# A two-layer decoder trunk on one core: squares of the last tiles, residual sums, two compression weights and one gate pair are placed differently

## Chip, core and metric

The kernel runs on one core of a Trainium2 chip. The metric is the device time of one execution, in microseconds (us). The core has TensorE (PE) for matrix products, VectorE (DVE), ScalarE (ACT) and GpSimd (POOL) for work on elements, and SyncE (SP), which here only starts DMA transfers. Each engine takes its instructions strictly in the order of its own queue; an instruction that must wait holds up all that stand behind it.

## What is computed

Two layers, each of two blocks with a norm before and after. Cut to what matters here:

```python
def hybrid_layer(x, ...):
    hn = rms_norm(x, norm_g[0])
    (nsa_q, k_c, v_c, ..., sb_q, sb_k, sb_v, merge_g) = split_columns(hn @ w_in)
    kc = compress_blocks(k_c, cmp_pe[0], cmp_w1[0], cmp_w2[0])   # gelu(flat @ w1) @ w2
    vc = compress_blocks(v_c, cmp_pe[1], cmp_w1[1], cmp_w2[1])
    y_nsa = nsa_attention(..., kc, vc, ...) @ w_nsa_o
    y_sb = stick_breaking_attention(...) @ w_sb_o
    gate = jax.nn.sigmoid(merge_g)
    mixed = (gate[..., :D_MODEL] * y_nsa + gate[..., D_MODEL:] * y_sb) @ w_out
    x = x + rms_norm(mixed, norm_g[1])
    hf = rms_norm(x, norm_g[2])
    ff = jnp.square(jax.nn.relu(hf @ w_ff1)) @ w_ff2
    return x + rms_norm(ff, norm_g[3])
```

The sequence has 512 positions, the model 1024 channels (eight tiles of 128), the feed-forward 4096, everything in float32.

## The kernel before

**Layout.** Activations lie with channels on the 128 partitions and the 512 positions along the row. Every large product is made of three: a float32 operand is split into a rounded part and a rest (`hi` and `lo`, in the names `w_hi`/`w_lo` for weights, `ah`/`al` and others for activations), and PE adds hi x hi, hi x lo and lo x hi (`three`, lines 185 to 187; `product`, lines 479 to 483).

**Weights.** `Weight` (line 146) loads 128x1024 values into `w_raw` (two buffers, DMA started by SP), ACT copies them rounded into `w_hi` (line 157), and the rest `w_lo` is made in one of two ways. As a rule POOL subtracts (line 162). With `sub="dma"`, ACT writes the negated rounded copy into `w_lo` (line 159) and a DMA issued from POOL adds the weight from memory onto it (line 160). `w_hi` and `w_lo` have four buffers.

**Compression.** `Compress.steps` (line 371) runs the first compression product in four weight portions for the keys (`ck`) and four for the values (`cv`); the bits of `CKM` and `CVM` in `PLAN` say which portions take the DMA way: 2 is portion 1 of `ck`, 1 is portion 0 of `cv`. `gelu` and `finish` follow; PE's products there are `cmp_t` (line 389) and `cmp_o` (line 409).

**What sets the order.** PE's order is the program's, written by hand: a filler (`Filler`, line 421) hands out a number of projection products between the steps of the attention (`PLAN` holds the numbers). On the other engines and queues a scheduler orders the instructions, under the limits of the buffer pools: a tile can be written when an earlier user of its buffer is done.

**Merge loop** (line 937). For each of the eight tiles m: two groups of products `y`, DVE multiplies each with its sigmoid (line 947), adds, and splits. The gates of tile 7 are projected inside this loop: at m = 1 both projections are added to the filler and all 48 products run.

**Tails** (`tail`, line 242). There are four: attention and feed-forward of each layer. A tail computes the last five of the eight tiles in two halves of 256 positions (`products`, `evacuate`). Each tile's squares are added by DVE into one sum (`sq_add`, line 237), which `rstd_fin` (line 209) sums over the partitions with a product by `ones` on PE (line 212) and turns into 1/rms (`Rpost`, lines 217 to 222). `residual` (line 282) makes for each of the eight tiles `pn` (DVE, line 291), the new `x` (line 292) and its split into `ah` (ACT, line 226) and `al` (DVE, line 227). The first three tails go on into the next block (`nxt` is set): their old `x` comes by DMA into buffers of the tag `sig` (line 277; six buffers, shared with gates and rope tables; the feed-forward tail has `x` in place), and PE starts the next block's first products, `head`, in pieces (`head_step`): k = 0 and 1 of the first half, then `rstd_fin` of the second half's `Rpost`, then the rest. The last tail has no next block and already gives PE one square tile apart (line 214).

Of the kernel before, what the change touches and what calls it, by code (L numbers as in the profile page):

```python
# [12 lines left out]
ALU = mybir.AluOpType  # L13
# [9 lines left out]
}  # L23
GN = 5
# [25 lines left out]
def layer_kernel(ctx, tc, xT, pos, gvec, tri, consts, smalls, w_in, w1, w_o, w_out, ff1, ff2, out):  # L50
# [11 lines left out]
    def big(tag, name, dt=F32):  # L62
        return sp.tile([P, T], dt, tag=tag, bufs=BUFS[tag], name=name)
# [145 lines left out]
    def rstd_fin(R, acc, c, more=None, tag="t"):  # L209
        n = c.stop - c.start  # L210
        ss = psum(tag, "ss")[:, 0:n]
        E.matmul(ss, ones, acc, start=True, stop=more is None)
        if more is not None:
            E.matmul(ss, ones, more, start=False, stop=True)
        v = half("var")
        y = R[:, c]
        S.activation(y, ss, AF.Ln, scale=1.0 / D, bias=eps_c)
        V.tensor_scalar(v, ss, 1.0 / D, EPS, ALU.mult, ALU.add)
        S.activation(y, y, AF.Exp, scale=-0.5)
        V.tensor_tensor(acc, y, y, ALU.mult)  # L220
        V.scalar_tensor_tensor(v, acc, -0.5, v, ALU.mult, ALU.mult)
        V.scalar_tensor_tensor(y, v, 1.5, y, ALU.add, ALU.mult)
# [19 lines left out]
    def tail(l, n, mixed, acc, load, acts, prev, src, nxt, head):  # L242


        group = range(KT - GN, KT)
        last_sq = []
        na = new_acts() if nxt is not None else None
        R = big("R", "Rpost")
        R2 = big("R", "Rpre") if nxt is not None else None
# [7 lines left out]
        def evacuate(hf, i):  # L257
            c = HALVES[hf]
            m, ps = group[i], pst[i][:, c]
            if prev is None:  # L260
                V.tensor_copy(mixed[m][:, c], ps)
            else:
                V.tensor_tensor(mixed[m][:, c], ps, prev[m][:, c], ALU.add)
            if nxt is None and (hf, i) == (1, GN - 1):
                last_sq.append(half("last_sq"))
                S.activation(last_sq[0], mixed[m][:, c], AF.Square)
            else:
                sq_add(acc[:, c], ps if prev is None else mixed[m][:, c], False, c, V)
            if nxt is None and hf == 1:
                S.activation(mixed[m][:, c], mixed[m][:, c], AF.Copy, scale=gcol(l, n, m))  # L270
# [11 lines left out]
        def residual(hf, xo):  # L282
            c = HALVES[hf]
            for k in range(KT):
                t = big("t", "pn")[:, 0:256]
                if nxt is None and hf == 1:
                    e = G if k in ENDP else V
                    e.tensor_tensor(t, mixed[k][:, c], R[:, c], ALU.mult)
                    (G if k == 5 else e).tensor_tensor(x[k][:, c], t, xo[k], ALU.add)
                else:  # L290
                    V.scalar_tensor_tensor(t, mixed[k][:, c], gcol(l, n, k), R[:, c], ALU.mult, ALU.mult)  # L291
                    (V if nxt is None and k in (1, 4, 7) else G).tensor_tensor(x[k][:, c], t, xo[k], ALU.add)
                if nxt is not None:
                    xsplit(na[k], x[k], gcol(nxt[0], nxt[1], k), c)
                else:
                    nc.sync.dma_start(out[:, k, c], x[k][:, c])
# [24 lines left out]
        if nxt is None:  # L321
            for m in range(KT - GN):
                S.activation(mixed[m][:, HALVES[1]], mixed[m][:, HALVES[1]], AF.Copy, scale=gcol(l, n, m))
            rstd_fin(R, acc[:, HALVES[1]], HALVES[1], last_sq[0])
            residual(1, xo)
            return None
        head_step(hd, na, HALVES[0], (0, 1))
        rstd_fin(R, acc[:, HALVES[1]], HALVES[1])
        residual(1, xo)
        a2 = squares(0), squares(1)  # L330
        head_step(hd, na, HALVES[0], range(2, KT))
# [139 lines left out]
    def layer(l, acts, R, heads):  # L471
# [465 lines left out]
        for m in range(KT):  # L937
            sig = sigs.pop(m)
            with tc.issue_after(last_exp.ins):
                for s in sig:  # L940
                    S.activation(s, s, AF.Sigmoid)
            wo, ys = early.pop(m, None) or (Weight(w_o[l, m]), {})
            for j, src in enumerate((o_nsa, o_sb)):
                ps, done = ys.get(j) or (psum("o", "y"), 0)
                for k in range(done, 4):
                    three(ps, wo, 4 * j + k, src[k], k == 0, k == 3)
                V.tensor_tensor(sig[j], ps, sig[j], ALU.mult)
            V.tensor_tensor(sig[0], sig[0], sig[1], ALU.add)
            tg = "Q" if m < 6 else "L"
            mh, ml = big(tg, f"mh{m}", F32R), big(tg, f"ml{m}", F32R)  # L950
            split(mh, ml, sig[0])
            merged.append((mh, ml))
            if m == PLAN["GA"]:
                fill.add(*gate_project(gates.pop(0)))
                fill.run(48)
        exp_table()

        mixed = [big("L", f"mix{m}") for m in range(KT)]
# [149 lines left out]
```

## Time and profile before

| | us |
|---|---|
| median of 3 runs | 1613.12 |
| lowest and highest of them | 1608.31 and 1613.18 |
| the profiled execution, its own time | 1610.72 |
| span of its profile, first to last instruction | 1608.8 |
| PE busy in the span | 1528.3 |
| DVE, ACT, POOL busy | 858.1, 748.9, 763.2 |

The profile gives, for each engine, when an instruction ran, and for a wait which instruction ended it. The granted clock (PEclk) is a share of TensorE's full speed: 1.00 is 2.4 GHz and 0.50 is 1.2 GHz. Times inside the execution count from the span's start. The stages in order, layer 0: projections and compression to about 120 us, attention to 335, merge and output product to 412, attention tail to 455, feed-forward to 785, its tail to 835; layer 1 repeats this.

### The profile page before, as it was taken

To read this page: it belongs to the slowest core of one execution; us is meant where nothing else is said; L and a number is where in the kernel's file an instruction comes from. 1 tells how busy PE (TensorE), PEld (TensorE's weight loads), DVE (VectorE), ACT (ScalarE), POOL (GpSimd) and SP (SyncE) were. 2 spreads that over 40 slices of the span, in tenths; PEclk is the share of its full clock that TensorE was granted. 3 is DMA by queue.
4 is the path that set the end of the run, shared out by engine and by line. 5 is a ranking of instruction groups with operands and counts; after the bars stand their busy time and mean duration, and the time that the engine had idled before them with its cause. 6 is when DMAs were issued, how large, how long until landed. Compare 5 with 4: busy or idle time off the path is not lost.

```text
span 1608.8 us, 20693 instructions
## 1 busy us (share of the span) xinstructions
PE 1528.3 (95%) x7810; PEld 1288.8 (80%) x7810; DVE 858.1 (53%) x1495; ACT 748.9 (47%) x1379; POOL 763.2 (47%) x527
## 2 busy tenths in 40 slices
PE   7789999999989999999988899999998999999996
PEld 5667778887978888888976787788878988888886
DVE  6788854355583232314698887534447713232245
ACT  6567754553352322324446777554444523232342
POOL 4574344535544444446546724444464444444452
PEclk9899999999999999999999999999999999999998
DMA  6443312224313233233334512122342132323321
GB/s 195 121 131 92 64 55 77 66 91 145 105 43 104 93 94 103 92 102 121 117 100 131 136 49 66 53 79 71 113 144 92 47 98 92 105 92 97 100 92 53
DMA packets 49331, 153.74 MB, mean 96 GB/s; under 512 B 5952, under 2 KB 12496, under 8 KB 49232
## 3 DMA queue, kind: packets, MB, share of 16 engines
q1 hardware_dynamic: 45888, 140.84, 27.2%
q0 software_dynamic: 3200, 11.55, 4.1%
q8 instruction: 61, 1.00, 0.3%
q14 instruction: 38, 0.31, 0.1%
q10 hardware_dynamic: 144, 0.03, 0.0%
HBM read 148.15 MB, written 4.26 MB: 95 GB/s over the span
## 4 chain that ended last, share of the span: by engine, by line
PE 78%; DVE 12%; ACT 2%; issue 2%; DMA 1%; POOL 1%; DVEq 0%; ACTq 0%; POOLq 0%
PE ff L186 12%; PE ff L187 12%; PE ff L185 12%; PE proj L479 5%; PE proj L483 5%; PE proj L481 5%; PE tail L187 2%; PE tail L186 2%; PE tail L185 2%; PE y L185 2%; PE p_t L720 2%; DVE P L690 2%; PE y L186 2%; PE y L187 2%; DVE pn L291 2%
## 5 line engine op out<-in xcount | busy, mean ns | idle before, releaser
L162 POOL TENSOR_TENSOR w_lo<-w_raw,w_hi 128x1024 fp32r<-128x1024 f32 x204 | 494.6, 2425 | 506.1 <-ACT w_hi L157 493.6
L157 ACT ACTIVATE w_hi<-w_raw 128x1024 fp32r<-128x1024 f32 x226 | 239.1, 1059 | 521.2 <-PE ff L186 371.7
L483 PE MATMUL proj<-ah,w_lo 128*128 128x512 f32 x496 | 198.7, 401 | 1.7 <-POOL w_lo L162 1.7
L479 PE MATMUL proj<-ah,w_hi 128*128 128x512 f32 x496 | 199.2, 402 | 0.9 <-ACT w_hi L157 0.9
L481 PE MATMUL proj<-al,w_hi 128*128 128x512 f32 x496 | 198.9, 401 | 0.0
L185 PE MATMUL ff<-ah,w_hi 128*128 128x512 f32 x448 | 174.3, 389 | 0.0
L186 PE MATMUL ff<-al,w_hi 128*128 128x512 f32 x448 | 174.3, 389 | 0.0
L187 PE MATMUL ff<-ah,w_lo 128*128 128x512 f32 x448 | 174.3, 389 | 0.0
L186 PE MATMUL ff<-hl,w_hi 128*128 128x512 f32 x432 | 168.2, 389 | 0.7 <-DVE hl L181 0.7
L185 PE MATMUL ff<-hh,w_hi 128*128 128x512 f32 x432 | 168.1, 389 | 0.0
L187 PE MATMUL ff<-hh,w_lo 128*128 128x512 f32 x432 | 168.1, 389 | 0.0
L181 DVE TENSOR_TENSOR hl<-relu,hh 128x512 fp32r<-128x512 f32 x64 | 106.8, 1673 | 83.7 <-ACT hh L180 83.5
L483 PEld LDWEIGHTS proj<-ah,w_lo 128*128 128x128 f32 x496 | 94.8, 191 | 19.0 <-POOL w_lo L162 2.1
L479 PEld LDWEIGHTS proj<-ah,w_hi 128*128 128x128 f32 x496 | 95.0, 192 | 17.4 <-ACT w_hi L157 1.1
L481 PEld LDWEIGHTS proj<-al,w_hi 128*128 128x128 f32 x496 | 95.0, 192 | 16.7
L1003 DVE TENSOR_TENSOR ffa<-ff,ffa 128x512 f32<-128x512 f32 x38 | 26.3, 692 | 151.3 <-PE ff L187 151.3
L185 PEld LDWEIGHTS ff<-ah,w_hi 128*128 128x128 f32 x448 | 84.1, 188 | 17.5
L187 PEld LDWEIGHTS ff<-ah,w_lo 128*128 128x128 f32 x448 | 84.1, 188 | 17.3
L186 PEld LDWEIGHTS ff<-al,w_hi 128*128 128x128 f32 x448 | 84.1, 188 | 17.3
L186 PEld LDWEIGHTS ff<-hl,w_hi 128*128 128x128 f32 x432 | 81.1, 188 | 17.9 <-DVE hl L181 1.1
L185 PEld LDWEIGHTS ff<-hh,w_hi 128*128 128x128 f32 x432 | 81.1, 188 | 17.0
L187 PEld LDWEIGHTS ff<-hh,w_lo 128*128 128x128 f32 x432 | 81.1, 188 | 16.6
(311 smaller groups left out, 3401.3 us busy)
## 6 DMA issues: line engine op xcount, KB each, us to landing
w_raw<-in_ff_dram SPq DMA_DIRECT2D x128, 512.0 KB, 3.5
w_raw<-in_w_in_dram SPq DMA_DIRECT2D x69, 512.0 KB, 3.6
w_lo<-in_w_in_dram POOLq DMA_DIRECT2D x18, 512.0 KB, 7.7
w_raw<-in_w_dram SPq DMA_DIRECT2D x16, 512.0 KB, 3.6
w_raw<-in_w_o_dram SPq DMA_DIRECT2D x16, 512.0 KB, 3.5
w_raw<-in_w_out_dram SPq DMA_DIRECT2D x16, 512.0 KB, 3.7
x<-in_xT_dram SPq DMA_DIRECT2D x8, 256.0 KB, 6.8
w_lo<-in_w_dram POOLq DMA_DIRECT2D x4, 512.0 KB, 7.0
```

The lines of the kernel that those rows point to most:

```text
L157: S.activation(h, raw, AF.Copy)
L162: (sub or G).tensor_tensor(l, raw, h.bitcast(F32), ALU.subtract)
L181: V.tensor_tensor(lo, src, hi.bitcast(F32), ALU.subtract)
L185: E.matmul(ps, w.hi(k), ah, start=first, stop=False)
L186: E.matmul(ps, w.hi(k), al, start=False, stop=False)
L187: return E.matmul(ps, w.lo(k), ah, start=False, stop=last)
L291: V.scalar_tensor_tensor(t, mixed[k][:, c], gcol(l, n, k), R[:, c], ALU.mult, ALU.mult)
L479: E.matmul(ps, w.hi(k), ah, start=(k == 0), stop=False)
L481: E.matmul(ps, w.hi(k), al, start=False, stop=False)
L483: E.matmul(ps, w.lo(k), ah, start=False, stop=(k == KT - 1))
L690: V.tensor_scalar(pr[h], pr[h], sm4[:, h:h + 1], None, ALU.mult)
L720: E.transpose(pt[:, P * h:P * h + P], pend[j][0][h][:, P * kt:P * kt + P], ident)
```

## The change

Four edits:

1. **Squares.** In the three tails with a next block, the squares of the last five tiles in the second half are no longer added by DVE. ACT writes them into buffers of the tag `sig` (two halves of 256 in each, so three buffers) and PE sums all five with a product by `ones` each, behind that of the sum so far.
2. **Residual sums.** The engine expression of the new `x` is turned round. For the last tail it selects the same engines as before; for the three tails with a next block all sixteen sums move from POOL to DVE.
3. **Compression weights.** `CKM` and `CVM` become 0: all eight portions have their `w_lo` from POOL's subtraction.
4. **Gate pair.** The first projection of gate 7 runs at m = 0, the second at m = 1, 24 products each.

```diff
-    ... "CKM": 2, "CVM": 1, ...
+    ... "CKM": 0, "CVM": 0, ...
@@ rstd_fin
         E.matmul(ss, ones, acc, start=True, stop=more is None)
-        if more is not None:
-            E.matmul(ss, ones, more, start=False, stop=True)
+        for i, m in enumerate(more or ()):
+            E.matmul(ss, ones, m, start=False, stop=i == len(more) - 1)
@@ tail
-        last_sq = []
+        last_sq, pairs = [], []
@@ evacuate
             if nxt is None and (hf, i) == (1, GN - 1):
                 last_sq.append(half("last_sq"))
                 S.activation(last_sq[0], mixed[m][:, c], AF.Square)
+            elif nxt is not None and hf == 1:
+                if i % 2 == 0:
+                    pairs.append(big("sig", "sq2"))
+                last_sq.append(pairs[-1][:, 256 * (i % 2) : 256 * (i % 2) + 256])
+                S.activation(last_sq[-1], ps if prev is None else mixed[m][:, c], AF.Square)
             else:
                 sq_add(acc[:, c], ps if prev is None else mixed[m][:, c], False, c, V)
@@ residual
-                    (V if nxt is None and k in (1, 4, 7) else G).tensor_tensor(x[k][:, c], t, xo[k], ALU.add)
+                    (G if nxt is None and k not in (1, 4, 7) else V).tensor_tensor(x[k][:, c], t, xo[k], ALU.add)
@@ end of tail
-            rstd_fin(R, acc[:, HALVES[1]], HALVES[1], last_sq[0])
+            rstd_fin(R, acc[:, HALVES[1]], HALVES[1], last_sq)
...
-        rstd_fin(R, acc[:, HALVES[1]], HALVES[1])
+        rstd_fin(R, acc[:, HALVES[1]], HALVES[1], last_sq)
@@ merge loop
-            if m == PLAN["GA"]:
+            if m == 0:
                 fill.add(*gate_project(gates.pop(0)))
-                fill.run(48)
+            if m < 2:
+                fill.run(24)
```

PE at the end of the attention tail of layer 0, between the second and the third step of `head`, before:

```order
L187 MATMUL head<-ah_3915,w_lo 128x256
L212 MATMUL ss<-macc,ones 128x256
L185 MATMUL head<-ah_3917,w_hi 128x256
L186 MATMUL head<-al_3918,w_hi 128x256
L187 MATMUL head<-ah_3917,w_lo 128x256
```

and the same place after:

```order
L187 MATMUL head<-ah_3913,w_lo 128x256
L212 MATMUL ss<-macc,ones 128x256
L214 MATMUL ss<-sq_4162,ones 128x256 x2
L214 MATMUL ss<-sq_4265,ones 128x256 x2
L214 MATMUL ss<-sq_4318,ones 128x256
L185 MATMUL head<-ah_3915,w_hi 128x256
```

Five products are new there; the numbers are only those of buffers. DVE in the same tail from the first half's `Rpost` on, before (`pn` is a normed tile, `x` the new residual, `mix` a tile copied out of the product's bank, `macc` the sum of squares):

```order
L291 SCALAR_TENSOR_TENSOR pn<-mix_3765,gv,Rpost 128x256
L291 SCALAR_TENSOR_TENSOR pn<-mix_3766,gv,Rpost 128x256
L291 SCALAR_TENSOR_TENSOR pn<-mix_3767,gv,Rpost 128x256
L291 SCALAR_TENSOR_TENSOR pn<-mix_3768,gv,Rpost 128x256
L237 TENSOR_TENSOR macc<-macc,sq 128x256
L291 SCALAR_TENSOR_TENSOR pn<-mix_3769,gv,Rpost 128x256
L227 SCALAR_TENSOR_TENSOR al_3914<-x_4122,gv,ah_3913 128x256
L261 COPY mix_3770<-tail_3971 128x256
L237 TENSOR_TENSOR macc<-macc,sq 128x256
L291 SCALAR_TENSOR_TENSOR pn<-mix_3770,gv,Rpost 128x256
L261 COPY mix_3771<-tail_3972 128x256
L227 SCALAR_TENSOR_TENSOR al_3916<-x_4123,gv,ah_3915 128x256
```

and after, from the third `x` on (four `pn`, a copy and two `x` stand ahead):

```order
L297 TENSOR_TENSOR x_4122<-pn,x_old 128x256
L297 TENSOR_TENSOR x_4123<-pn,x_old 128x256
L296 SCALAR_TENSOR_TENSOR pn<-mix_3767,gv,Rpost 128x256
L261 COPY mix_3768<-tail_3969 128x256
L296 SCALAR_TENSOR_TENSOR pn<-mix_3768,gv,Rpost 128x256
L227 SCALAR_TENSOR_TENSOR al_3912<-x_4120,gv,ah_3911 128x256
L296 SCALAR_TENSOR_TENSOR pn<-mix_3769,gv,Rpost 128x256
L296 SCALAR_TENSOR_TENSOR pn<-mix_3770,gv,Rpost 128x256
L297 TENSOR_TENSOR x_4124<-pn,x_old 128x256
L297 TENSOR_TENSOR x_4125<-pn,x_old 128x256
L227 SCALAR_TENSOR_TENSOR al_3914<-x_4121,gv,ah_3913 128x256
L261 COPY mix_3769<-tail_3970 128x256
```

The sums of squares have left DVE, the sums `x` stand there, and the second `al` stands behind eight `pn`, six `x` and two copies. Behind the last row follow the seventh `x`, an `al`, the eighth `x`, two `al`, a copy and three `al`. POOL in the compression stage of layer 0, before:

```order
L343 TENSOR_TENSOR qr<-q,cosT 128x512
L160 DMA w_lo<-in_w_dram 128x1024
L143 TENSOR_TENSOR qpl<-q,qph 128x512
L162 TENSOR_TENSOR w_lo<-w_raw,w_hi 128x1024 x4
L343 TENSOR_TENSOR qr<-q,cosT 128x512
L160 DMA w_lo<-in_w_dram 128x1024
L143 TENSOR_TENSOR qpl<-q,qph 128x512
L162 TENSOR_TENSOR w_lo<-w_raw,w_hi 128x1024 x2
```

and after:

```order
L348 TENSOR_TENSOR qr<-q,cosT 128x512
L162 TENSOR_TENSOR w_lo<-w_raw,w_hi 128x1024
L143 TENSOR_TENSOR qpl<-q,qph 128x512
L162 TENSOR_TENSOR w_lo<-w_raw,w_hi 128x1024 x4
L348 TENSOR_TENSOR qr<-q,cosT 128x512
L162 TENSOR_TENSOR w_lo<-w_raw,w_hi 128x1024
L143 TENSOR_TENSOR qpl<-q,qph 128x512
L162 TENSOR_TENSOR w_lo<-w_raw,w_hi 128x1024
```

Each DMA issue has become a subtraction in its place. Two further moves follow from the buffers of the tag `sig`: on SP the old `x` of a tail's second half is loaded behind the feed-forward weights instead of among the output weights, and the rope tables of layer 1 are set up at the end of layer 0's feed-forward tail instead of in its attention tail.

## Rows read from the trace of the kernel before

**Rows 1.** Busy time by stage: stage; its us; PE, PEld, DVE, ACT, POOL; PEclk, DMA.

```profile
425.00:460.00 35.00, 28.98 (x223) 28.34 (x222) 29.44 (x47) 14.83 (x33) 19.65 (x18) 0.90 0.20 65
```

**Rows 2.** PE's waits, whole span: waiting <- releaser: us in total, times, longest.

```profile
PE cmp_h L379 <- DMA w_lo<-in_w_dram: 10.4, 3, 8.8
PE ss L212 <- DVE macc L237: 8.2, 2, 4.1
...
PE ss L212 <- DVE facc L237: 5.7, 2, 5.0
```

**Rows 3.** Timeline of PE in the tails: start, us, instruction, [idle before <- releaser].

```profile
444.39 0.39 PE L186 MATMUL head<-al,w_hi 128*128 128x256 f32 x1 [1.90 <-DVE al L227]
444.62 0.28 PE L187 MATMUL head<-ah,w_lo 128*128 128x256 f32 x1
...
445.68 0.28 PE L187 MATMUL head<-ah,w_lo 128*128 128x256 f32 x1
450.08 0.79 PE L212 MATMUL ss<-macc,ones 128*128 128x256 f32 x1 [4.12 <-DVE macc L237]
...
809.66 0.79 PE L212 MATMUL ss<-facc,ones 128*128 128x256 f32 x1 [4.95 <-DVE facc L237]
```

**Rows 4.** Short stretches, columns as in rows 1: read PE busy and PEclk.

```profile
388.90:392.30 3.40, 3.40 (x10) 2.67 (x9) 2.03 (x2) 1.58 (x2) 1.16 (x2) 0.52 0.62 208
...
450.10:453.70 3.60, 3.60 (x15) 3.42 (x16) 2.73 (x8) 2.93 (x8) 0.24 (x1) 0.51 0.59 186
...
808.70:815.50 6.80, 5.84 (x25) 5.66 (x26) 6.26 (x16) 4.51 (x13) 1.05 (x2) 0.50 0.25 80
```

**Rows 5.** Chain of work in the attention tail: start, us, engine, result, line.

```profile
429.00 0.43 PE ss L212 x2
...
440.46 2.40 DVE macc L237
...
444.74 0.40 DVE al L227
...
446.02 0.33 DVE macc L237
...
447.55 2.15 DVE al L227
...
450.08 1.22 PE ss L212 x2
```

**Rows 6.** Timeline of DVE: the ends of the first half's 1/rms.

```profile
431.56 0.43 DVE L222 SCALAR_TENSOR_TENSOR Rpost<-var,Rpost 128x256 f32<-128x256 f32 x1
...
792.45 0.42 DVE L222 SCALAR_TENSOR_TENSOR Rpost<-var,Rpost 128x256 f32<-128x256 f32 x1
```

**Rows 7.** Timeline of POOL in the attention tail: two weight splits.

```profile
440.18 2.40 POOL L162 TENSOR_TENSOR w_lo<-w_raw,w_hi 128x1024 fp32r<-128x1024 f32 x1
...
446.89 2.52 POOL L162 TENSOR_TENSOR w_lo<-w_raw,w_hi 128x1024 fp32r<-128x1024 f32 x1
```

**Rows 8.** Timeline of ACT in the attention tail: the third weight's rounding.

```profile
444.37 1.05 ACT L157 ACTIVATE w_hi<-w_raw 128x1024 fp32r<-128x1024 f32 x1
```

**Rows 9.** Timeline of PE in the compression stages of both layers.

```profile
67.71 0.47 PE L379 MATMUL cmp_h<-w_lo,bhl 128*64 128x256 f32 x1 [8.83 <-DMA w_lo<-in_w_dram]
96.21 0.28 PE L409 MATMUL cmp_o<-cmp_ht,sml 128*64 128x32 f32 x1 [4.82 <-issue]
...
856.04 0.28 PE L378 MATMUL cmp_h<-w_hi,bhl 128*64 128x256 f32 x1
...
890.55 0.32 PE L409 MATMUL cmp_o<-cmp_ht,sml 128*64 128x32 f32 x1 [2.89 <-DVE cmp_ht L400]
```

**Rows 10.** Timeline of PE and ACT in the merge loop of layer 0.

```profile
388.06 0.47 PE L185 MATMUL y<-onh,w_hi 128*128 128x512 f32 x1 [2.40 <-DVE sig L947]
...
383.26 1.06 ACT L157 ACTIVATE w_hi<-w_raw 128x1024 fp32r<-128x1024 f32 x1 [4.84 <-DMA w_raw<-in_w_out_dram]
```

**Rows 11.** DMA issues of the page: transfer, count, KB each, median us to landing.

```profile
x<-in_xT_dram SPq DMA_DIRECT2D x8, 256.0 KB, 6.8
```

2 rows, old and new, of the table PLAN are left out of this document.

## Prediction

> **What bounds the kernel now.** I read the stages first, then PE's waits, then the timelines around them. PE is busy 1528.3 of 1608.8 us, so time is won where PE stands idle or runs at half its clock, and an edit on another engine counts only if PE waits for that engine there. The list of waits [rows 2] names three that the change can touch: the second half's `ss` waiting for DVE's sum of squares in the two attention tails (8.2 us in two waits) and in the feed-forward tail with a next block (4.95 of 5.7 us), and the compression waiting for a weight that comes by a DMA (8.8 us once).
>
> The attention tail of layer 0 is the clearest [rows 1]: of 35 us PE works 29 and DVE 29.4. Its chain [rows 5] runs from the first half's `ss` through DVE to the second half's `ss`. In it two sorts of DVE rows stand beside each other: an `al` takes 0.40 and a `macc` 0.33, but one `macc` takes 2.40 and one `al` 2.15. On POOL a weight split runs from 440.18 for 2.40 and another from 446.89 for 2.52 [rows 7]: the long DVE rows lie on them. I call this a lock: a DVE instruction on two tiles of SBUF that meets a split costs 2.0 to 2.4 us in place of 0.33 to 0.40. PE pays twice [rows 3]: 1.90 us before the second step of `head`, and 4.12 before `ss`. Behind that wait PE runs at 0.51 of its clock until 453.7 [rows 4], the 1.2 GHz level; for 2.4 us after `ss` has ended this costs another 1.2. The feed-forward tail has one wait of 4.95 and the low clock till 815.5.
>
> **Tails: squares and residual sums.** These two edits act on one chain and are costed together. DVE loses five adds of 0.33 behind Rpost and gets sixteen sums of 0.33 from POOL. POOL loses the sums, so its splits now run when their rounded weight is ready, not behind the sums. PE gets five pairs of products by `ones`, 0.43 us each at full clock (`ss` x2 [rows 5]), six with the old one: 2.6 us. At the low clock one pair took 1.22 [rows 5]. ACT writes the squares itself.
>
> Rpost is ready at 432.0 [rows 6]. From there DVE's new order puts eight `pn`, two `al`, two copies and six `x` up to the second `al`: 10 x 0.40 + 8 x 0.33 = 6.7, so 438.7 without locks. PE is ready for that step at 442.5 (444.39 less 1.90). Each split that meets the queue adds about 2.4. Two give 443.5, three 445.9. PE then needs 1.57 for the step (to 445.96, where the wait of 4.12 begins) and 2.6 for the six sums. The last square comes behind the eighth `x`, 1.4 + 0.8 us after the second `al`, and is no later than PE. So `ss` ends at 446.7, 447.7 or 450.05 with no, two or three locks. Before, it ended at 451.3 with 1.2 of low clock behind it, 452.5 in effect. The gain is 5.8, 4.8 or 2.45. If the low clock comes as in the merge loop (a 3.4 us stretch at 0.52 behind a wait of 2.4 [rows 4, 10], so 1.7 lost), three locks leave 0.75. The third weight's rounding ran at 444.37 on ACT [rows 8], so its split came at the end of this stretch, but nothing on POOL holds the first two back any more. **I take 1.7** for each of the two attention tails, between 2.45 and 0.75, since all three splits fall between Rpost and `ss` in the trace too; the ends are 0.75 and 5.8.
>
> A rule speaks against moving the sums. The rows show 2.40 in place of 0.33 on a split. The Trainium skill, page "SBUF — State Buffer", section "Who interferes with whom", says that a DVE instruction with two SBUF inputs contends with a GpSimd instruction that reads SBUF, and that the loser of the shared ports blocks for the whole instruction. The trace agrees with it (2.40). By that rule the sums, which meet POOL's splits on DVE now, gain nothing over the `macc` that they replace, and three splits keep their full price; if the second of them blocked nothing, the tail would gain 2.4 more.
>
> In the feed-forward tail Rpost is ready at 792.9 [rows 6]; ten instructions of 0.40 and ten of 0.33 and a short wait for a bank give the second `al` at 800.6, and 803.0 with one lock, while PE needs it at 803.1: covered. PE ends the step at 804.7 (809.66 less 4.95). With a lock the last square comes at 807.6 and `ss` ends at 808.0. Before it ended at 810.9, then 4.6 us at 0.50 until 815.5 [rows 3, 4], 2.3 lost: 813.2 in effect. **Gain 5** (6.0 without a lock, 2.9 if the low clock stays).
>
> What is late next: the second half's residual. PE has 72 products of half 0 left behind `ss`, 0.12 us apart (from 444.62 to 445.68 are nine steps [rows 3]): 8.6 us. DVE needs 2.6 for Rpost (from 429.43 to 432.0 [rows 5, 6]) and, up to the first `al`, six `pn`, four `x` and five sums of the next norm: 7 x 0.40 + 9 x 0.33 = 5.8, together 8.4. It just fits, with three of the sums standing in pauses of Rpost.
>
> The old `x` of the second half now comes later on SP, behind the weights of the feed-forward, and its last piece only when PE has read the third square buffer. Transfers of 256 KB of `x` took 6.8 us to land [rows 11], and the pieces are read from 3 us after `ss` on, the last at the end of 9 us of DVE work. I cost it at nothing; its cover is PE's 8.6 us, and without it a piece costs up to 4. The rope tables set up later are used 25 us afterwards: nothing.
>
> **Compression weights.** In layer 0 PE waits 8.83 for the DMA's weight from 58.9 on, and 37.3 us later `cmp_o` starts at 96.21 behind another wait of 4.82. In layer 1 no such wait stands there: from 856.3 to `cmp_o` at 890.55 are 34.2 us [rows 9]. So the whole wait is worth 37.3 − 34.2 = 3.1, since the chain before `cmp_o` is late anyway. Against it stand two splits of 2.40 more per layer, which can lock DVE in that chain: 4.8 at worst. **I take +2 in layer 0** (−1.7 to +5.9, the latter 8.83 less the 2.89 which remains in layer 1) **and 0 in layer 1** (−4.8 to +2.9). The two ACT copies and POOL's DMA issues that go are hidden, as no PE wait there ends on them.
>
> **Gate pair.** 24 products move in front of three products of `y`. The wait of 2.40 in the merge loop at 388.06 follows ACT's rounding of an output weight at 383.26, which had waited 4.84 for its DMA [rows 10]; that stays. 0 (−1 to +2.4).
>
> **Sum.** 1.7 + 5 + 1.7 + 2 + 0 + 0 = 10.4. The profiled execution took 1610.7, 2.4 less than the median 1613.1; the three runs and it have the mean 1611.3. From that: 1600.9, so 1601. Not all terms go to the same end: lows of 0.75, 2.9, 0.75 and 1 give 5.4, highs of 2.45, 6, 2.45 and 4.5 give 15.4, so 1596 to 1606 for this case.
>
> **Rivals.**
> (a) *Slower.* The sums by PE run at 1.2 GHz. With three locks PE waits before `ss` at 447.5, as it did before 450.08, and the clock falls there as it fell in every tail of the trace. Then six pairs take 6 x 1.22 = 7.3 in place of 1.22, `ss` ends at 454.8, and with 1.2 of low clock behind it the tail ends 3.5 later than before. In both attention tails: +7, with nothing won in the other tail and in compression: 1618. It decides where the waits ahead of the sums leave PE at 1.2 GHz when the first pair starts, as the one pair of 1.22 before. For it: each wait of 2.4 or more in these rows has a low clock behind it. Against it: the wait would be split in two shorter ones. 0.09.
> (b) *Given back.* One lock in the second half makes its first `al` 2.2 late; in three tails 6.6, and compression gives nothing: 10.4 − 8.6 = 1.8, so 1609.5. For it: 8.4 against 8.6. Against it: in the trace the weight splits have ended by then. 0.17.
> (c) *No locks.* POOL is free, so the first two splits run before Rpost is ready: 5.8 + 6 + 5.8 + 2 = 19.6, so 1591.5. The rounding at 444.37 speaks against it for the third. 0.15.
> (d) *The DMA wait comes back in full* (8.8), with the tails as forecast and 2.9 in layer 1: 8.4 + 8.8 + 2.9 = 20.1, so 1591. `cmp_o`'s own wait speaks against it. 0.05.
> That the gate pair does nothing is part of the forecast, which has 0.54.
>
> **How the numbers follow.** A measurement of this kernel can tell about 0.3%, 4.8 us, from no change, so faster is below 1608.3. The forecast and (c) and (d) are faster: 0.74; (b) is the same: 0.17; (a) is slower: 0.09. The range leaves out (a) and about half of (c) and (d): 1592 to 1611.
>
> **What would show it.** Right: in the attention tails the waits of 1.90 and 4.12 become one of 1 to 3.4 us before the second step and nearly none before `ss`; six pairs of `ss` take 2.6 us; the clock stays at 1.00 or falls for less than 3.4 us. DVE's rows of 2 us and more stand on `w_lo` splits, of `x` or `pn` now. The feed-forward tail's 4.95 shrinks below 3. The wait at 67.71 is gone, and `cmp_o` comes about 2 us earlier, with a longer wait before it. Wrong: `ss` rows of 1.22 each (a), a wait of `head` in the second half for `al` or an old `x` (b), splits that end before Rpost (c), or `cmp_o` later than 96.2. The forecast as a whole falls if the tails together give less than 4 us.

## The result and the profile after

| | before | after |
|---|---|---|
| median of 4 runs, us | 1612.82 | 1599.49 |
| lowest to highest | 1608.31 to 1613.18 | 1598.86 to 1601.39 |
| ratio to before, 95% interval | | 0.9932 [0.9913, 0.9950] |
| span of the profiled execution | 1608.8 | 1599.6 |

The kernel is faster by 0.7%, some 13 us by the medians and 9.2 by the two profiled spans. The forecast was 1601, in a range of 1592 to 1611. The time was right; two of the terms that it is made of were not, and the experiments below show a third thing that the prediction never asked: what the squares and the sums are worth apart.

Where the time went can be read from PE alone, by the starts of the first product of each stage in the two traces. "Attention tail" runs from its first product to the first product of the feed-forward; "feed-forward tail" from its first product to the first `head` product behind the next norm's second `ss`; compression from the first product of `head` (layer 0) or from that point (layer 1) to the second `cmp_o`; merge from there to the attention tail.

| stage, us | before | after | difference | forecast |
|---|---|---|---|---|
| to the end of compression, layer 0 | 125.41 | 126.76 | +1.35 | −2 |
| attention and merge, layer 0 | 280.76 | 282.62 | +1.86 | 0 |
| attention tail, layer 0 | 61.65 | 58.35 | −3.30 | −1.7 |
| feed-forward tail, layer 0 | 59.68 | 54.05 | −5.63 | −5 |
| compression, layer 1 | 92.34 | 92.68 | +0.34 | 0 |
| attention and merge, layer 1 | 278.91 | 278.03 | −0.88 | 0 |
| attention tail, layer 1 | 61.67 | 58.36 | −3.31 | −1.7 |

The feed-forward products themselves (299.3 and 300.2 us) and the last tail (30.1, to its last `ss`) stand as before, within 0.3. PE in the tails after the change (start, us, instruction, [idle before <- releaser]; compare [rows 3]):

```profile
448.30 0.39 PE L186 MATMUL head<-al,w_hi 128*128 128x256 f32 x1 [2.37 <-DVE al L227]
449.72 0.60 PE L212 MATMUL ss<-macc,ones 128*128 128x256 f32 x2
450.15 2.32 PE L214 MATMUL ss<-sq,ones 128*128 128x256 f32 x10
...
804.91 0.60 PE L212 MATMUL ss<-facc,ones 128*128 128x256 f32 x2
805.34 2.32 PE L214 MATMUL ss<-sq,ones 128*128 128x256 f32 x10
```

The waits of 4.12 and 4.95 in front of `ss` are gone. The one in front of the second step of `head` is 2.37 in place of 1.90. The six sums take 2.4 us, from the first one's start to that of the next `head` (452.13). The stage of [rows 1], moved by the 3.4 us by which the tail now starts later, reads:

```profile
428.40:463.40 35.00, 32.63 (x261) 32.08 (x260) 29.97 (x64) 15.89 (x37) 7.25 (x3) 1.00 0.24 76
```

PE is busy for 32.6 of the 35 us in place of 29.0, and at the full clock (1.00 in place of 0.90). What DVE does between Rpost and that `al`, with POOL's three splits beneath:

```profile
435.32 1.67 DVE L296 SCALAR_TENSOR_TENSOR pn<-mix,gv,Rpost 128x256 f32<-128x256 f32 x4
...
437.24 3.30 DVE L297 TENSOR_TENSOR x<-pn,x_old 128x256 f32<-128x256 f32 x4
...
441.19 2.60 DVE L296 SCALAR_TENSOR_TENSOR pn<-mix,gv,Rpost 128x256 f32<-128x256 f32 x1
...
444.11 3.08 DVE L296 SCALAR_TENSOR_TENSOR pn<-mix,gv,Rpost 128x256 f32<-128x256 f32 x2
...
447.78 0.47 DVE L227 SCALAR_TENSOR_TENSOR al<-x,gv,ah 128x256 fp32r<-128x256 f32 x1
```

```profile
436.79 2.46 POOL L162 TENSOR_TENSOR w_lo<-w_raw,w_hi 128x1024 fp32r<-128x1024 f32 x1 [13.58 <-ACT w_hi L157]
441.10 2.41 POOL L162 TENSOR_TENSOR w_lo<-w_raw,w_hi 128x1024 fp32r<-128x1024 f32 x1 [1.85 <-ACT w_hi L157]
444.13 2.38 POOL L162 TENSOR_TENSOR w_lo<-w_raw,w_hi 128x1024 fp32r<-128x1024 f32 x1 [0.62 <-ACT w_hi L157]
```

Each split has one stretched row of DVE on it. From the end of Rpost (435.28) to the end of the second `al` (448.25) are 13.0 us, where the prediction had 13.9 with three locks.

### The profile page after: what moved, and what is told of

Its sections match the earlier page's. It is cut to its first block, busy times and chain, and to the rows that moved or that the text cites. A ratio compares the mean times of both kernels' runs of the same rounds, so it can differ in the third digit from the quotient of the medians.

```text
span 1599.6 us, 20724 instructions
## 1 busy us (share of the span) xinstructions
PE 1530.3 (96%) x7840; PEld 1289.9 (81%) x7840; DVE 847.1 (53%) x1528; ACT 744.3 (47%) x1375; POOL 731.5 (46%) x479
## 4 chain that ended last, share of the span: by engine, by line
PE 78%; DVE 9%; POOL 3%; DMA 2%; issue 2%; ACT 2%; DVEq 0%; POOLq 0%; ACTq 0%
PE ff L186 12%; PE ff L185 12%; PE ff L187 12%; PE proj L488 5%; PE proj L484 5%; PE proj L486 5%; PE tail L185 2%; PE tail L187 2%; PE tail L186 2%; POOL w_lo L162 2%; PE y L185 1%; PE y L186 1%; PE p_t L725 1%; PE y L187 1%; PE head L186 1%
## 5 line engine op out<-in xcount | busy, mean ns | idle before, releaser
L162 POOL TENSOR_TENSOR w_lo<-w_raw,w_hi 128x1024 fp32r<-128x1024 f32 x208 | 504.3, 2425 | 585.5 <-ACT w_hi L157 573.4
```

The costliest lines, as they stand in the source:

```text
L162: (sub or G).tensor_tensor(l, raw, h.bitcast(F32), ALU.subtract)
```

## The experiments

Each was timed in five rounds beside the kernel before on the same chip; the chips differ between runs (medians of the kernel before from 1611.2 to 1612.8), so the ratios are the fairer comparison and medians of two rows can be 1 to 2 us off. The tails of each, in us of its profiled execution, are the best view of what an edit does:

| kernel | median | ratio to before | attention tail 0 | feed-forward tail | attention tail 1 |
|---|---|---|---|---|---|
| before | 1612.82 | 1 | 61.65 | 59.68 | 61.67 |
| whole change | 1599.49 | 0.9932 [0.9913, 0.9950] | 58.35 | 54.05 | 58.36 |
| e1: two tail edits | 1602.32 | 0.9940 [0.9928, 0.9952] | 59.98 | 54.05 | 60.04 |
| e2: weights alone | 1610.22 | 0.9996 [0.9987, 1.0006] | 61.31 | 59.48 | 61.76 |
| e3: gate pair alone | 1611.87 | 1.0000 [0.9990, 1.0010] | 61.71 | 59.67 | 61.83 |
| e4: squares alone | 1595.24 | 0.9902 [0.9889, 0.9915] | 57.19 | 55.34 | 57.19 |
| e5: sums alone | 1611.53 | 1.0000 [0.9990, 1.0010] | 61.26 | 59.60 | 61.72 |
| e6: squares, sums in the feed-forward tail | 1594.87 | 0.9887 [0.9873, 0.9900] | 57.15 | 54.05 | 57.16 |
| e7: as e6, and late sums | 1592.74 | 0.9878 [0.9864, 0.9891] | 56.59 | 54.06 | 56.60 |
| e8: whole, head weight by DMA | 1598.65 | 0.9920 [0.9907, 0.9934] | 60.03 | 54.05 | 58.28 |
| e9: whole, three weights by DMA | 1591.88 | 0.9876 [0.9861, 0.9891] | 55.67 | 54.06 | 55.67 |
| e10: whole, early sums on POOL | 1592.98 | 0.9886 [0.9869, 0.9902] | 56.59 | 54.06 | 56.60 |
| e11: e1 with the wait filled | 1599.14 | 0.9919 [0.9904, 0.9934] | 58.26 | 54.06 | 58.26 |
| e12: e9 with two more changes | 1592.37 | 0.9888 [0.9871, 0.9906] | 54.37 | 56.59 | 54.37 |

### One part alone: tails, weights, gate pair

e1 undoes the weights and the gate pair; e2 and e3 do one of them each on the kernel before:

```diff
 e2 on the kernel before
-"CKM": 2, "CVM": 1
+"CKM": 0, "CVM": 0
 e3 on the kernel before
-            if m == PLAN["GA"]:
+            if m == 0:
                 fill.add(*gate_project(gates.pop(0)))
-                fill.run(48)
+            if m < 2:
+                fill.run(24)
```

> The kernel before with the two edits of the tails only (squares summed by PE, residual sums on DVE). Theory T, read off the places of the two traces: the three tails give 3.3 + 5.6 + 3.3 = 12.2 us, so about 1600.6 against 1612.8, as fast as the whole change or 1 to 3 us faster, because the weights and the gate pair give nothing. Rival R, the prediction's terms: the tails give 8.4 (1604.4), and what is missing to the whole change comes from the weights.

> The kernel before with only the compression weights changed (all eight split on POOL). Theory T: the wait of 8.83 for the DMA's weight goes, but cmp_o of layer 0 comes 1 to 2 us later than at 96.2 and the stage's end (second cmp_o at 130.8) about 1.4 later; layer 1 0.3 later: 1.7 us slower, 1614.5. Rival R: cmp_o comes about 2 us earlier, 1610.8.

> The kernel before with only the gate pair in two portions. Theory T: in the trace of the whole change the merge loop of layer 0 lost 1.9 and that of layer 1 won 0.9; if the pair does that, the same differences stand here, 1 us slower (1613.8). Rival N: they come from when an output weight's transfer lands, by chance or through the stages before; then the pair changes nothing (1612.8 within 1) and the wait in the loop varies from run to run.

The tails alone give 0.9940, nearly all of the change. The weights and the gate pair alone can't be told from no change.

**Weights.** PE's waits in layer 0 of e2, from the one that replaces the 8.83 of [rows 9] to `cmp_o`:

```profile
59.70 0.33 PE L379 MATMUL cmp_h<-w_lo,bhl 128*64 128x256 f32 x1 [1.71 <-POOL w_lo L162]
65.17 0.77 PE L479 MATMUL proj<-ah,w_hi 128*128 128x512 f32 x1 [4.45 <-DVE sig L642]
67.16 0.79 PE L483 MATMUL proj<-ah,w_lo 128*128 128x512 f32 x1 [0.80 <-POOL w_lo L162]
83.07 0.34 PE L389 MATMUL cmp_t<-cst,cmp_hs 64*128 64x64 f32 x2 [3.15 <-ACT cmp_hs L382]
93.57 0.50 PE L673 MATMUL s<-K1w,xr 128*128 128x512 f32 x1 [2.16 <-DVE mx L679]
97.06 0.60 PE L409 MATMUL cmp_o<-cmp_ht,sml 128*64 128x32 f32 x4 [1.46 <-issue]
```

The one wait for the DMA is gone, and the six waits add up to 13.7, nearly as much as those before (8.83 and 4.82 in [rows 9] and two of 0.86 and 0.40 between them, 14.9). PE meets the DVE and ACT chains of the same stage earlier and waits for them instead. `cmp_o` starts at 97.06, 0.85 later than in [rows 9], or 0.47 counted from the first product of `head`, which starts 0.38 later in e2. Over all kernels of this study the way to the second `cmp_o` of layer 0 took 123.8 to 125.4 us with the old weights (nine executions, mean 124.6) and 124.9 to 126.8 with the new ones (five, mean 126.1); in layer 1, 92.3 to 93.7 (eight, mean 93.2) and 91.7 to 93.1 (six, mean 92.4). By the means the edit costs about 1.5 us in layer 0 and gives about 0.8 in layer 1; the ranges overlap, and e2's own 124.9 is below the 125.4 of the kernel before.

The clock shows where the loss in layer 0 comes from. These are the stretches of this stage with the low clock, two in the kernel before and three in e2 (columns as in [rows 1]):

```profile
61.10:71.30 10.20, 3.59 (x12) 3.20 (x13) 5.39 (x8) 5.26 (x11) 6.26 (x4) 0.50 0.70 189
95.20:102.10 6.90, 5.89 (x21) 4.89 (x22) 5.75 (x7) 1.67 (x5) 6.90 (x5) 0.51 0.27 81
```

```profile
63.40:70.30 6.90, 4.33 (x10) 2.98 (x11) 4.58 (x7) 3.33 (x9) 4.68 (x2) 0.51 0.22 78
83.90:87.30 3.40, 3.40 (x10) 2.65 (x9) 3.34 (x5) 1.74 (x4) 1.46 (x1) 0.50 0.32 92
94.20:101.00 6.80, 5.34 (x21) 4.11 (x20) 5.85 (x14) 4.10 (x12) 6.63 (x5) 0.50 0.25 91
```

Both kernels have 17.1 us at 1.2 GHz, but before, most of the first stretch lay under the wait of 8.83, where it cost nothing: PE worked at the low clock for 9.5 us in the first kernel and for 13.1 us in e2. Half of that time is lost. The nine executions with the old weights lose 3.9 to 5.1 us of this stage in that way (mean 4.6), the five with the new ones 6.5 to 8.3 (mean 7.1), and these ranges don't meet; PE's idle time is much the same (means 18.9 and 18.3). In layer 1 the losses overlap widely (2.5 to 8.0 and 4.1 to 5.7).

**Gate pair.** The wait in the merge loop of layer 0 (2.40 in [rows 10]) in the whole change, in e1 without the pair, and in e3 with the pair alone:

```profile
390.26 0.77 PE L185 MATMUL y<-onh,w_hi 128*128 128x512 f32 x1 [3.06 <-DVE sig L952]
```

```profile
388.25 0.62 PE L185 MATMUL y<-onh,w_hi 128*128 128x512 f32 x1 [3.06 <-DVE sig L952]
```

```profile
386.96 0.47 PE L185 MATMUL y<-onh,w_hi 128*128 128x512 f32 x1 [2.20 <-DVE sig L947]
```

It doesn't go with the pair. In the whole change ACT's rounding before it had waited 5.56 for its weight's transfer, 4.84 before. The wait follows that transfer: over the 28 merge loops of all kernels it took 3.4 to 5.3 us from its issue to its landing, and the wait is always 2.2 us shorter, from 1.2 to 3.1. In layer 1 the transfer took 3.4 to 3.7 us in the nine kernels in which PE sums all five squares and 4.4 to 4.7 in the other five, so the 0.9 us that layer 1's merge gains may belong to the squares. Why the transfer is faster or slower wasn't settled.

**Tails and clock.** e1 has the same order in its tails as the whole change and the same wait (2.29 and 2.37), yet takes 1.6 us longer in each attention tail. The stretch of its six sums (start:end us; PE, PEld, DVE, ACT, POOL; granted clock, DMA):

```profile
446.40:450.50 4.10, 4.10 (x14) 3.31 (x13) 2.26 (x6) 0.88 (x3) 0.00 (x0) 0.58 0.71 225
```

The clock is mostly at its 1.2 GHz level, 0.58 on average, and the sums take 4.1 us in place of 2.4. Of e1's five executions three took 1602.3 to 1602.8 at a mean granted clock of 0.983 or 0.984, and two 1599.3 and 1599.9 at 0.986; that fits two tails of 1.6 us, though only the profiled execution (1602.4) shows where its clock was low. So the rival (a) of the prediction is real, but smaller: 1.6 us a tail, in some executions. It took for each of six pairs the 1.22 us that one pair's rows span in [rows 5], ends included; at the low clock e1's products start 0.43 apart, 0.85 a pair, and the last four of the twelve are back at the full clock.

### Squares alone, sums alone

e4 keeps the squares' edit and leaves the sums on POOL; e5 is the reverse:

```diff
 e4 on e1
-(G if nxt is None and k not in (1, 4, 7) else V).tensor_tensor(x[k][:, c], t, xo[k], ALU.add)
+(V if nxt is None and k in (1, 4, 7) else G).tensor_tensor(x[k][:, c], t, xo[k], ALU.add)
```

> The kernel before with only the squares of the second half summed by PE, the residual sums left on POOL. Theory T: the waits for macc and facc (4.1, 5.0, 4.1) went because the sum left DVE, so this alone gives the larger part: the feed-forward tail in full (5.6) and the attention tails 2 to 4 each, 1601 to 1603. Rival S: the sums x on POOL stand behind the splits there, so the eighth square of x's chain and the al come late: the attention tails give under 1 each and the whole 5 to 7 us, 1606 to 1608.

> The kernel before with only the residual sums of the three tails moved to DVE; the squares stay with DVE's adds. Theory D (from the tails of the two kernels before this one: with the sums on DVE the attention tails took 1.2 to 2.8 us longer than with them on POOL, the feed-forward tail 1.3 less): the sums lengthen DVE's queue ahead of the second al and of the adds of squares, so 2 to 6 us slower than before, 1613.5 to 1617.5. Rival P, the prediction's reading: DVE is rid of POOL's sums as contenders, so 0 to 3 us faster.

The squares alone give 0.9902, more than both edits (e1, 0.9940) and more than the whole change (whose interval just meets e4's; e1's does not). The sums alone give nothing, 1.0000; the expected loss did not come. e4's PE has no wait of `head` in the first half at all, and `ss` waits 0.18:

```profile
442.15 0.59 PE L212 MATMUL ss<-macc,ones 128*128 128x256 f32 x2
442.58 1.89 PE L214 MATMUL ss<-sq,ones 128*128 128x256 f32 x8
444.66 0.70 PE L214 MATMUL ss<-sq,ones 128*128 128x256 f32 x2 [0.18 <-ACT sq L271]
```

DVE's rows of e4 up to the second `al` say why:

```profile
433.33 2.30 DVE L296 SCALAR_TENSOR_TENSOR pn<-mix,gv,Rpost 128x256 f32<-128x256 f32 x1
435.55 0.96 DVE L227 SCALAR_TENSOR_TENSOR al<-x,gv,ah 128x256 fp32r<-128x256 f32 x1
436.43 0.95 DVE L296 SCALAR_TENSOR_TENSOR pn<-mix,gv,Rpost 128x256 f32<-128x256 f32 x1
437.31 0.96 DVE L227 SCALAR_TENSOR_TENSOR al<-x,gv,ah 128x256 fp32r<-128x256 f32 x1
```

Rpost ends there at 430.39 and the second `al` at 438.27: 7.9 us in place of 13.0. POOL makes the `x` beside DVE:

```profile
431.00 1.80 POOL L297 TENSOR_TENSOR x<-pn,x_old 128x256 f32<-128x256 f32 x2 [12.65 <-DVE pn L296]
432.75 2.59 POOL L162 TENSOR_TENSOR w_lo<-w_raw,w_hi 128x1024 fp32r<-128x1024 f32 x1
435.31 3.55 POOL L297 TENSOR_TENSOR x<-pn,x_old 128x256 f32<-128x256 f32 x4
```

The `al` stands behind six `pn` and no `x`, and one split lies in its way in place of three, though most rows are longer (0.95 in place of 0.48) where they stand on POOL's sums. With the adds of squares still on DVE it is different: in e5 the `al` are in time and all the wait stands in front of `ss`.

```profile
449.24 1.22 PE L212 MATMUL ss<-macc,ones 128*128 128x256 f32 x2 [5.31 <-DVE macc L237]
```

So what the sums cost depends on the other edit. Before, the adds of squares ended last and hid it; once they are gone, the `al` is the next limit, and the sums on DVE delay exactly that.

### Where the sums belong

```diff
 e6 on e4: the engine of the new x
-V if nxt is None and k in (1, 4, 7) else G
+V if src is None and nxt is not None or nxt is None and k in (1, 4, 7) else G
 e7 on e4
+V if nxt is not None and (hf == 1 or src is None) or nxt is None and k in (1, 4, 7) else G
```

> Squares summed by PE in the three tails; the residual sums on DVE in the feed-forward tail alone, on POOL in the attention tails. Theory D: 4.5 + 5.6 + 4.5 = 14.6 us from the tails, 1.3 more than with all sums on POOL: about 1594 where the squares alone gave 1595.2. Rival E: the 1.3 us of the feed-forward tail are of the one execution that was profiled; 1595 to 1596.

> As the kernel with the sums on DVE in the feed-forward tail, and in the attention tails the sums of the second half on DVE too; those of the first half stay on POOL. Theory D: what the sums on DVE cost is the second al of the first half; behind ss they cost nothing, and PE's products of the second half no longer wait for POOL's sums (18.5 us from ss to the next norm's sum, 17.45 with the sums on DVE): 1 us less in each attention tail, about 1592. Rival F: DVE is late behind ss too, so PE waits for al in the second half: no gain or up to 2 us slower than the kernel with the sums only in the feed-forward tail.

In the feed-forward tail the sums on DVE do help: 54.05 in place of e4's 55.34, also in e6. In the attention tails they help only behind `ss`: e7's tails take 56.6 in place of 57.2, half of the 1 us expected. PE's longest wait in the second half of that tail falls from 0.39 to 0.24:

```profile
453.58 0.38 PE L186 MATMUL head<-al,w_hi 128*128 128x256 f32 x1 [0.24 <-DVE al L227]
```

e7 has the lowest time of these, 0.9878, though its interval overlaps that of e6. e10 makes the same move in the whole change, the first half's sums going back to POOL:

> The whole change, but in the attention tails the residual sums of the first half go back to POOL. Theory D: as in the kernel with squares and late sums, without the new weights and gate pair, the attention tails take 56.6 us each (58.4 in the whole change): 3.5 us less than the whole change, 1596, and 0 to 3 above 1592.7 as the weights and the gate pair give. Rival G: weights and gate pair give 2 us with this tail too: under 1592.

It gives 1592.98, and the attention tails 56.6 as in e7: the place of sixteen adds (eight in each attention tail) is worth 3.5 us by the profiled tails. By the medians e10 is 6.5 below the whole change, but that is not shown to come from the adds: in the profiled executions layer 0's attention and merge alone differ by 4.5 (282.6 and 278.1), with a wait in the merge loop of 3.06 and 1.31 and 6.8 us of low clock behind the first and none behind the second. With weights and gate pair (e10) or without (e7) makes no difference that can be told.

### The locks

The splits on DVE's way could be taken out while the sums stay on DVE. e8 tried the wrong weight, the last one of `head`; e9 the right ones, the first three of the feed-forward's own products:

```diff
 e8 on the whole change, in the attention tails
-        def start(self):
+        def start(self, sub=None):
             while len(self.ws) < 4:
-                self.load()
+                self.load(sub)
-        hd = head.start() if nxt is not None else None
+        hd = head.start(None if src is None else "dma") if nxt is not None else None
 e9 on the whole change
-                dense(ps, Weight(ff1[l, c * KT + m]), acts)
+                dense(ps, Weight(ff1[l, c * KT + m], sub="dma" if c == 0 and m < 7 else None), acts)
```

> The whole change, but in the two attention tails the fourth weight of head gets its rest by a DMA that adds in place of a split on POOL. Theory L: the third lock (two pn in 3.08 us where 0.8 would do) goes, the second al comes 2.3 us earlier, PE's wait of 2.36 ahead of it falls under 0.5 in both attention tails: 1595 against 1599.5. Rival Q: the queue itself (eight pn and six x ahead of that al) holds it, and the DMA's weight lands no earlier than it is needed: the wait stays over 1.5 and the time within 1 us of 1599.5.

> The whole change, but the three weights whose splits met DVE in the attention tails (they belong to the feed-forward product, 25 us ahead of their use) get their rest by a DMA that adds. Theory L: without those splits eight pn, six x and two al need 6.7 us from Rpost on, the second al is there before PE wants it, the waits of 2.36 go in both attention tails (under 0.3 each) and the clock stays at 1.00: 4.5 us less than the whole change, 1595. Rival Q: DVE's queue without locks is still too long, a wait over 1 us stays: within 1.5 us of 1599.5.

In e8 the three splits stood where they had been: the weight of `head` is split at 420.8 in the whole change, before Rpost. The wait stayed at 2.35. But that execution shows the clock's part within one kernel: the six sums of its two attention tails follow waits of 2.35 and 2.29, and run at 0.60 in the first and 1.00 in the second.

```profile
445.20:449.20 4.00, 4.00 (x14) 3.27 (x13) 2.18 (x6) 0.80 (x3) 0.00 (x0) 0.60 0.66 221
1229.70:1232.20 2.50, 2.50 (x15) 2.22 (x14) 2.31 (x6) 0.93 (x3) 0.00 (x0) 1.00 0.66 193
```

e9's DVE has the same instructions as in the whole change; the first rows keep their order, and one copy and the seventh `x`, 0.7 us in all, now stand ahead of the second `al`:

```profile
430.66 1.67 DVE L296 SCALAR_TENSOR_TENSOR pn<-mix,gv,Rpost 128x256 f32<-128x256 f32 x4
...
432.59 1.42 DVE L297 TENSOR_TENSOR x<-pn,x_old 128x256 f32<-128x256 f32 x4
...
434.66 0.47 DVE L296 SCALAR_TENSOR_TENSOR pn<-mix,gv,Rpost 128x256 f32<-128x256 f32 x1
...
435.45 0.87 DVE L296 SCALAR_TENSOR_TENSOR pn<-mix,gv,Rpost 128x256 f32<-128x256 f32 x2
...
437.58 0.47 DVE L227 SCALAR_TENSOR_TENSOR al<-x,gv,ah 128x256 fp32r<-128x256 f32 x1
```

The four `x` take 1.42 in place of 3.30, the `pn` 0.47 in place of 2.60, the two `pn` 0.87 in place of 3.08. Together 6.2 us; Rpost to the second `al` is 7.4 us in place of 13.0, with the two further rows in it (6.7 in the prediction without locks and without these rows). PE has no wait above 0.1 between the tail's first product and the feed-forward, the clock is 1.00 throughout, and both attention tails take 55.7. The two tails give 5.4 us. The median is 1591.88, 7.6 us below the whole change, of which the part outside the tails isn't shown to come from this edit (layer 0's attention and merge took 278.1 here as in e10). It is the lowest median of all, but its interval overlaps those of e4, e6, e7, e10 and e12. The Trainium skill, page "SBUF — State Buffer", section "Who interferes with whom", says that DMA has ports of its own. The trace agrees: the three adding DMAs are issued at 433.55, 436.43 and 439.67 and land by 449.74, and no row of DVE from Rpost until then takes more than 0.49 us.

### The clock behind the wait

```diff
 e11 on e1, in the attention tails
-        head_step(hd, na, HALVES[0], (0, 1))
+        head_step(hd, na, HALVES[0], (0,))
+        d = psum("t", "ss")[:, 0:256]
+        for i in range(5):
+            E.matmul(d, ones, mixed[0][:, HALVES[0]], start=i == 0, stop=i == 4)
+        head_step(hd, na, HALVES[0], (1,))
```

> The kernel with the tails' two edits only, and in the attention tails five products by ones on a tile that is long ready, whose sum nobody reads, between the first and the second step of head, where PE waits 2.3 us. Theory K: the clock falls behind that wait because PE stands still; filled with work the clock stays at 1.00 in both attention tails, the six sums take 2.4 us in place of 4.1, and the tails 58.4 in place of 60.0: 1.6 us less for each tail in which the clock fell, 1599 to 1600 against 1602.3. Rival M: the clock falls in some executions whatever PE does there; the sums take 4 us in at least one tail and the time stays at 1602.

PE works through the wait, the granted clock is 1.00 in both tails, the six sums take 2.4 us, and the tails take 58.3: as K expected, 3 us under e1 by the medians (the two intervals overlap) and 3.5 by the profiled tails. It isn't proof that the wait pulls the clock down: with the wait unfilled three of six profiled tails (both of the whole change and one of e8) kept 1.00 as well, so two filled ones at 1.00 could be chance.

### A version on top of the best

```diff
 e12 on e9
-            elif nxt is not None and hf == 1:
+            elif nxt is not None and hf == 1 and i > 2:
...
-"CKM": 0, "CVM": 0
+"CKM": 2, "CVM": 1
-sub="dma" if PLAN[("CKM", "CVM")[self.i]] >> u & 1 else None
+sub="dma" if self.l == 0 and PLAN[("CKM", "CVM")[self.i]] >> u & 1 else None
```

> The kernel of the last three weights by DMA (1591.9), with two more changes: PE sums only the squares of the last two tiles and DVE adds those of the three before them (DVE has 0.5 to 1.3 us of idle time there now); and layer 0 has its two compression weights by the DMA way again, layer 1 not. Theory A: three pairs of products of 0.4 go in each of three tails (3.6 us), and layer 0's way to the second cmp_o takes 124.6 in place of 126.1 as in the kernels with the old weights (1.4): 1587. Rival B: the adds on DVE wait for ACT's squares, push the second al or the sum past the time PE wants it, and a wait of 1 us or more ahead of ss comes back in the tails: 1590 or more.

Two of the three tails and layer 0 gained at least what was expected, and other stages took it back. The attention tails took 54.4, 1.3 us less each, and layer 0's way to the second `cmp_o` 124.3 in place of 126.2. But the feed-forward tail lost 2.5. POOL still has a split there, and that locks DVE (the timelines of POOL, DVE, ACT and PE in that tail):

```profile
793.18 3.41 POOL L162 TENSOR_TENSOR w_lo<-w_raw,w_hi 128x1024 fp32r<-128x1024 f32 x1
```

```profile
794.28 2.60 DVE L227 SCALAR_TENSOR_TENSOR al<-x,gv,ah 128x256 fp32r<-128x256 f32 x1
...
797.33 0.41 DVE L263 TENSOR_TENSOR ffa<-tail,ffa 128x256 f32<-128x256 f32 x1
```

```profile
797.77 0.42 ACT L271 ACTIVATE sq<-ffa 128x256 f32<-128x256 f32 x1 [1.53 <-DVE ffa L263]
```

```profile
798.24 0.70 PE L214 MATMUL ss<-sq,ones 128*128 128x256 f32 x2 [2.09 <-ACT sq L271]
```

The locked `al` holds up the tile that the last square is made of. With five pairs PE was busy until that square was there; with two it waits 2.09, and the clock falls behind it (0.64 from 800 to 804). The merge loops were 1.3 longer each as well, with waits of 2.84 and 2.49 in place of 1.42 and 1.23: the transfer of the output weight took 5.1 and 4.7 us in place of 3.6 and 3.4, for a reason that isn't settled. So e12 is no faster than e9.

## Why the prediction was right, and where it was not

**What bounds the kernel, tails.** Right in kind. The waits for `macc` and `facc` went, one wait in front of the second step of `head` stayed, and the stretched rows of DVE stand on the splits, on `pn` and `x` as it said. e9 is the proof of the locks: without the splits the queue needs 7.4 us with two rows more (forecast 6.7 without them), with the three 13.0 (13.9).

**Size of the attention tails.** The term was mis-sized: 3.3 measured, 1.7 forecast. It was taken between 2.45 and 0.75, the lower for a clock that falls. In this execution the clock did not fall, the `al` came 0.9 sooner than the sum of three locks, and the second step and the six sums took 1.42 and 2.41 in place of 1.57 and 2.6. These three add 1.2 to the 2.45; 0.3 goes the other way, since the prediction let the old `ss` end 1.22 after its start, while PE went on with `head` 0.66 after it, at the low clock. In e1 the clock fell and the gain was 1.7, so 1.7 fits only the case that the profile of the whole change did not show.

**The third weight.** "The third weight's rounding ran at 444.37" was right, but I did not say whose weights the splits were. They are the feed-forward's, whose first product comes 27 us after the last of these splits. Taking them off POOL gave 5.4 us in the two attention tails (e9), keeping the first half's sums on POOL 3.5 (e10).

**Feed-forward tail.** 5 forecast, 5.63 measured, covered as it said: the second `al` came in time with one lock ahead of it (a `pn` of 2.62 at 794.72), and the tail's second split hit the third `al` (2.61 at 803.52). The last square, forecast for 807.6 (which its numbers give only with one more lock of 2.4), was ready at 806.9.

**Two edits costed as one.** Here the step itself failed, though the sum did not show it. The squares and the sums were put on one chain and priced together, since both change DVE's queue. Alone, the squares give 13.3 us by the tails (e4), and the sums, once the squares have gone, cost 1.2 us in an attention tail at full clock and 2.8 where it falls (the whole change and e1 against e4). The rival in which the change gives back part of its gain was sought behind `ss`; it stood ahead of it, in the eight `pn` and six `x` of the order that the prediction had quoted. Without the sums' move in the first half the change took 1593 (e10).

**Behind `ss`.** 8.4 us of DVE against PE's 8.6 was the forecast: PE shows no wait above 0.1 there in the whole change, so the late sums and the later loads of the old `x` cost nothing.

**Weights.** Wrong in sign for layer 0: +2 forecast, about −1.5 in the mean of fourteen executions; in layer 1 0 forecast, about +0.8. The step that failed is the comparison with layer 1: it took the 3.1 us by which layer 0's stretch was longer for the price of the DMA wait. The rows of e2 show that the idle time of the stretch nearly stays (13.7 against 14.9) and only changes its releaser, and that PE then works at 1.2 GHz for 13.1 us in place of 9.5, which the prediction did not count at all. Whether the two more splits a layer cost something besides isn't shown. Together with the gate pair, forecast at 0 and measured at 1.0000 [0.9990, 1.0010], these parts cancel the underestimate of the tails: 12.2 − 1.7 − 1.0, less 0.4 elsewhere, make the 9.1 us between the two traces. The sum of 10.4 came out near the 9.1 by luck: the tails were 3.8 too low, the weights 3.7 too high.

**Open.** What makes the transfer behind the wait in the merge loops take 3.4 or 5.3 us, and when the clock falls behind a wait of 2.3 us.

## What to carry to other kernels

Price each edit by itself, and again with the other edits in place: an edit that is free while another limit ends last can be the limit once that one is gone (the sums on DVE: 0 alone, a loss of 4 us by the tails and 7 by the medians with the squares, from e1 and e4). When DVE rows of one shape come in two lengths, look for the POOL row beneath, ask whose work it is and when that is wanted, and move it or give it to a DMA. A long wait that goes is worth what the next limit of the stretch leaves; add up all waits of the stretch before and after, not the one, and look at how much of PE's work falls into the low clock.

## What was not expected of the hardware

The same wait of 2.3 us in front of the same products is followed by a granted clock of about 0.6 in some tails and 1.00 in others, even within one execution (e8: 0.60 and 1.00), at a price of 1.6 us a tail. A long wait can hide the low clock: 17.1 us of it cost 4.7 us where a wait of 8.8 covered most of the first stretch, and 6.5 where shorter waits left PE more to do in it (compression of layer 0, before and e2). A split of 2.4 us on POOL can cost DVE nearly its whole length: three of them stretched DVE's rows by 6.2 us, and its queue took 13.0 us with them and 7.4 without.
